# Stick-breaking attention on one core: the scan reads its own score tile, the constant's bank goes to the projections

## Chip, cores, metric

The kernel runs on 1 core of one Trainium2 chip. The metric is the device time of one execution in microseconds (us). PE is TensorE, DVE is VectorE, ACT is ScalarE, POOL is GpSimd, SP is SyncE.

## What is computed

One decoder layer: a modulated RMSNorm, one input projection, an RWKV-7 group and a stick-breaking attention group of 8 heads x 64, an output projection, a final RMSNorm. Sequence 2048, width 1024. The change lies in the attention:

```python
z = jnp.einsum('bhqd,bhkd->bhqk', q_blk, k).astype(jnp.float32) * scale
mask = k_pos[None, :] < q_pos[:, None]
log_1m = jnp.where(mask, jax.nn.log_sigmoid(-z), 0.0)
after = lax.cumsum(log_1m, axis=3, reverse=True) - log_1m
attn = jnp.where(mask, jnp.exp(jax.nn.log_sigmoid(z) + after), 0.0)
return jnp.einsum('bhqk,bhkd->bhqd', attn.astype(v.dtype), v)
```

With u = sigmoid(-z) and s = sigmoid(z) the weight of a key is s times the product of u over the later allowed keys.

## The kernel before

The program has three stretches: a start (modulation, the normed input h in two float16 parts, the first projections), the attention, and the RWKV group with the output projection. The attention and the RWKV stretch are separate scheduling contexts. In the first, a list scheduler sets the order on every engine from its own estimate of durations; each engine then executes its list strictly in order.

The attention has 16 steps n = 4j + b: j is a pair of heads, b a block of 512 queries. Step n has 8(b + 1) *score tiles* of 128 queries x up to 512 keys, and as many *turns*; 320 of each in all. For a score tile (`scores`): two matmuls write z into one of three PSUM banks (lines 492, 493); ACT makes u and s from z (496, 497); DVE scans u from the last key to the first (505, 508), a running product whose start is in the extra column `u[:, nk]`; POOL multiplies s by the shifted result (509). In a diagonal tile the last 128 keys are masked: POOL zeroes s above the diagonal (502), and the scan takes the maximum with a constant, 1 where the key is not allowed. For a turn (`turn`, `weigh`): PE transposes up to four 128 x 128 pieces into one of two `tr` banks (521), ACT and DVE split them in a high and a low part (525, 526), and two matmuls add both, weighted with v, to the `av` bank (539, 540). Score tiles run 5 ahead of turns, and `weigh` 3 behind them.

The scan has a second operand, `data1`: the constant `dmask`, which stands in a PSUM bank of its own for the whole attention. With `op1=ALU.bypass` its values are ignored.

Beside the attention, `fill` computes the projections that later steps need: k, q and the gates (24 matmuls with 512 columns each, lines 356 to 358, tiles psk, psq, psg, pss), v (96 matmuls with 128 columns, lines 368 to 370, psv). `_merge` interleaves the two jobs by estimated durations; the scheduler then moves instructions further. All projections of the attention write into the one `mm` bank. It is free again when ACT and DVE have taken the sum out (lines 419 and 420 for k, 405 and 406 for q, 432 and 433 for v, 441 and 442 for a gate). Ahead of the attention `mm_ps` hands out the three z banks instead.

PSUM has eight banks here: mm 1, z 3, tr 2, av 1, dmask 1.

Of the kernel before, what the change touches and what calls it, by code (L numbers as in the profile page):

```python
# [7 lines left out]
F32 = mybir.dt.float32  # L8
# [4 lines left out]
AF = mybir.ActivationFunctionType  # L13
ALU = mybir.AluOpType
# [4 lines left out]
P = 128  # L19
D = 1024  # L20
KB = D // P
TB = 512
# [32 lines left out]
def _merge(*jobs):  # L55
    _run(_side(*jobs))
# [32 lines left out]
def trunk(nc, a, out):  # L89
# [3 lines left out]
    PE, V, A, G, DMA = nc.tensor, nc.vector, nc.scalar, nc.gpsimd, nc.sync  # L93
# [5 lines left out]
    base = -(-nc.sbuf_base // 32) * 32  # L99
# [5 lines left out]
    def dram(name, shape):  # L105
        return nc.dram_tensor(name, shape, F32, kind="Internal").ap()
# [3 lines left out]
    sm = stage.enter_context(tc.tile_pool(name="small", bufs=2))  # L110
    pp = stage.enter_context(tc.tile_pool(name="ps", bufs=2, space=PSUM))

    NM = [1, 3, 2]
    early = [True]

    def mm_ps(name="mm"):
        if early[0]:
            return z_ps(name)
        return pp.tile([P, TB], F32, tag="mm", bufs=NM[0], name=name)

    def z_ps(name="z"):
        return pp.tile([P, TB], F32, tag="z", bufs=NM[1], name=name)

    def tr_ps(name="tr"):
        return pp.tile([P, TB], F32, tag="tr", bufs=NM[2], name=name)

# [84 lines left out]
    for e in range(2):  # L211
# [4 lines left out]
        for m in range(8):  # L216
# [16 lines left out]
                    op0=ALU.bitwise_and)  # L233
# [117 lines left out]
    def inproj(w, b, name):  # L351
        wh, wl = w[0], w[1]
        ps = mm_ps(name)
        for k in range(KB):
            with tc.issue_after(pace[0]) if pace[0] is not None else nullcontext():
                PE.matmul(ps, wh[:, k], hth[b][:, k], start=k == 0, stop=False)  # L356
            PE.matmul(ps, wh[:, k], htl[b][:, k], start=False, stop=False)  # L357
            PE.matmul(ps, wl[:, k], hth[b][:, k], start=False, stop=k == KB - 1)  # L358
            yield 0.65
        return ps  # L360
# [114 lines left out]
    def step(n):  # L475
        if n not in steps:
            b = n % NB
            steps[n] = ([(h, kb) for h in range(2) for kb in range(b, -1, -1)], {}, {}, {})
        return steps[n]

    def scores(n, i, sb):
        j, b = divmod(n, NB)
        groups, att, carry, _ = step(n)
        qt = qst[n]
        gi, q = divmod(i, 4)
        h, kb = groups[gi]
        kt = kst[NB * j + kb]
        diag = kb == b
        nk = (q + 1) * P if diag else TB
        qs = slice(q * P, (q + 1) * P)  # L490
        z = z_ps()
        PE.matmul(z[:, 0:nk], qt[:, h, 0, qs], kt[:, h, 0:nk], start=True, stop=False)  # L492
        PE.matmul(z[:, 0:nk], qt[:, h, 1, qs], kt[:, h, 0:nk], start=False, stop=True)  # L493
        u = sb.tile([P, TB + 1], F32, tag="u", bufs=NU, name="u")
        s = sb.tile([P, TB], F32, tag="s", bufs=NS, name="s")
        A.activation(out=u[:, 0:nk], in_=z[:, 0:nk], func=AF.Sigmoid, scale=-0.125)  # L496
        A.activation(out=s[:, 0:nk], in_=z[:, 0:nk], func=AF.Sigmoid, scale=0.125)  # L497
        ur = u[:, 0:nk][:, ::-1]
        mr = dmask[:, TB - nk:TB][:, ::-1]
        if diag:  # L500

            G.affine_select(out=s[:, nk - P:nk], in_=s[:, nk - P:nk], pattern=[[-1, P]], compare_op=ALU.is_gt,
                            fill=0.0, base=0, channel_multiplier=1)
            G.memset(u[:, nk:nk + 1], 1.0)
            V.tensor_tensor_scan(out=ur, data0=ur, data1=mr, initial=u[:, nk:nk + 1], op0=ALU.mult, op1=ALU.max)  # L505
        else:
            G.tensor_copy(out=u[:, nk:nk + 1], in_=carry[h, q][:, 0:1])
            V.tensor_tensor_scan(out=ur, data0=ur, data1=mr, initial=u[:, nk:nk + 1], op0=ALU.mult, op1=ALU.bypass)  # L508
        G.tensor_tensor(out=s[:, 0:nk], in0=s[:, 0:nk], in1=u[:, 1:nk + 1], op=ALU.mult)  # L509
        carry[h, q] = u  # L510
        att[gi, q] = s
        return 0.45 * nk / TB
# [60 lines left out]
    def attend(n, sb):  # L573

        p0 = seq.index((n, 0))
        p1 = p0 + 8 * (n % NB + 1)
        ahead = LEAD if n % NB else 0
        if n % NB == 1 or n == 0:
            for p in range(p0, p0 + LEAD):
                yield scores(*seq[p], sb)  # L580
        for p in range(p0, p1):
            if p + LEAD < min(p1 + ahead, len(seq)):
                yield scores(*seq[p + LEAD], sb)
            held.append(turn(*seq[p], sb))
            yield 0.43
            if len(held) > LAG:
                weigh(sb, *held.pop(0))
            yield 0.43
        if n == NST - 1:
            while held:  # L590
                weigh(sb, *held.pop(0))
# [41 lines left out]
    def fill(n, sb):  # L633

        j, b = divmod(n, NB)
        end = j == NB - 1
        if n < 2:
            m = n + 2
        else:
            m = n + 1 if 2 < n < NST - 1 else None  # L640
        new = b == 3 and not end
        if b == 0 and j > 0:
            yield from w_split("g", j)
        if b == 2:
            yield from w_split("r", j)
            w_load("z" if end else "k", 0 if end else j + 1)
        if b == 3:
            yield from w_split("z" if end else "k", 0 if end else j + 1)
            w_load("rk" if end else "q", 0 if end else j + 1)
        gates = [("g", 0)], [("g", 1)], [("g", 2), ("g", 3), ("r", 0)], [("r", 1), ("r", 2), ("r", 3)]  # L650
        gates = [proj_g(kind, j, gb, sb) for kind, gb in gates[b]]
        if m is not None:
            yield from proj_k(m)
            if new:
                yield from gates.pop(0)
                yield from w_split("q", j + 1)
                w_load("v", j + 1)
            yield from proj_q(m)
            if new:
                yield from gates.pop(0)  # L660
                yield from w_split("v", j + 1)
                w_load("g", j + 1)
            yield from proj_v(m)
        if j > 0:
            yield from combine(j - 1, b, sb)
        if n == NST - 1:
            for i in range(4):
                yield from proj_z(i, sb)
                if gates:
                    yield from gates.pop(0)  # L670
                if i < 3:
                    yield from w_split(("rk", "rr", "rv")[i], 0)
                if i < 2:
                    w_load(("rr", "rv")[i], 0)
        for g in gates:
            yield from g
        if b == 1:
            w_load("r", j)

    def fill_work(n):  # L680
        b = n % NB
        if n == NST - 1:
            return 5.2 * 7 + 1.5
        return 5.2 * ((4, 4, 6, 6)[b] - 3 * (n == 2)) + 0.9 * (n > 3) + (0.2, 0, 0.2, 0.6)[b]

    dts = []
    early[0] = False
    with tc.tile_pool(name="sb", bufs=2) as sb:

        dmask = pp.tile([P, TB], F32, tag="dmask", bufs=1, name="dmask")  # L690
        dm = sb.tile([P, TB], F32, tag="ot", bufs=1, name="dm")
        G.memset(dm, 0.0)
        G.affine_select(out=dm[:, TB - P:TB], in_=dm[:, TB - P:TB], pattern=[[-1, P]], compare_op=ALU.is_gt,
                        fill=1.0, base=0, channel_multiplier=1)
        A.activation(out=dmask, in_=dm, func=AF.Copy)
        for n in range(NST):
            b = n % NB
            _merge((attend(n, sb), 8.6 + 10.48 * b), (fill(n, sb), fill_work(n)))
            if n == 1:

                zeros = sb.tile([P, TB], F32, tag="ot", bufs=1, name="zeros")
                G.memset(zeros, 0.0)
                for i in range(2):
                    dts.append(dram(f"dt{i}", [2, 2, 8, 65, 64]))
                    for m in range(2):
                        for h in range(2):
                            DMA.dma_start(out=dts[i][m, h].rearrange("c s t -> s c t")[0:64],
                                          in_=zeros[0:64].rearrange("p (c d) -> p c d", c=8))
# [12 lines left out]
    pp = stage.enter_context(tc.tile_pool(name="ps", bufs=2, space=PSUM))  # L721
    NM[:] = [3, 2, 2]
    rwk = stage.enter_context(ExitStack())
# [598 lines left out]
```

## Time and profile before

| | |
|---|---|
| runs | 1924.12 us median of 3 (1922.18 to 1925.9) |
| the profiled execution | 1919.86 us, span 1918.1 us |
| busy in the span | PE 1699.1 us (89%), DVE 1380.4 (72%), ACT 859.7 (45%), POOL 774.4 (40%) |
| attention (137 to 1043 us) | 906 us: PE busy 837, DVE 676, ACT 535, POOL 470 |
[...]

PE counts as busy while a matmul is in its pipeline, so that neighbours overlap; the cost of a matmul in a dense row is the distance between starts. The waits view gives, for each pair of a waiting instruction and the one that released it, the idle time in all, how often, and the longest.

### The profile page before, as it was taken

The numbers are of one execution on the slowest core, as the hardware profiler recorded it, in microseconds if no ns is written. First come the engines' busy times: TensorE is split into PE (matmuls) and PEld (weight loads), VectorE is DVE, ScalarE is ACT, GpSimd is POOL, SyncE is SP. The second block draws the span as 40 slices with busy tenths as digits, with TensorE's granted clock in tenths as the row PEclk, the third lists the DMA queues.
The fourth block names the chain that finished last, engine by engine and source line by source line (L and its number), as shares of the span: only waits on it lengthen the run. The fifth ranks groups of instructions, "written<-read, shape, count | busy, mean of one in ns | idle before, by whom it ended". The sixth has DMA issues, their size and how long they took to land. (4 is left out here: it accounts for less than half of the span.)

```text
span 1918.1 us, 38809 instructions
## 1 busy us (share of the span) xinstructions
PE 1699.1 (89%) x14816; PEld 1164.2 (61%) x14816; DVE 1380.4 (72%) x2871; ACT 859.7 (45%) x1706; POOL 774.4 (40%) x1114
## 2 busy tenths in 40 slices
PE   1879978999899998999997888898899998989998
PEld 1546655666565665667654455665565655667886
DVE  8967697678785778768766557878777777765543
ACT  0556576456564666546644333333332333422221
POOL 3615465356553556445444123233233322223322
PEclk9989999999999999999989989999999999999999
DMA  8341201222122221132111523322332333335442
GB/s 296 112 144 45 70 25 45 64 75 64 42 56 75 61 67 41 51 79 69 54 45 39 154 49 86 69 62 77 77 80 77 86 78 104 80 92 169 149 138 88
DMA packets 210408, 159.93 MB, mean 83 GB/s; under 512 B 113247, under 2 KB 171820, under 8 KB 210222
## 3 DMA queue, kind: packets, MB, share of 16 engines
q1 hardware_dynamic: 209220, 155.31, 28.8%
q8 instruction: 117, 1.92, 0.4%
q10 hardware_dynamic: 1002, 2.13, 0.4%
q14 instruction: 69, 0.57, 0.1%
HBM read 94.48 MB, written 44.04 MB: 72 GB/s over the span
## 5 line engine op out<-in xcount | busy, mean ns | idle before, releaser
L509 POOL TENSOR_TENSOR s<-s,u 128x512 f32<-128x512 f32 (+2 forms) x320 | 306.0, 964 | 219.6 <-ACT s L497 99.7
L526 DVE TENSOR_TENSOR al<-tr,ah 128x512 fp32r<-128x512 f32 (+1 forms) x320 | 187.3, 598 | 98.0 <-ACT ah L525 97.2
L508 DVE TENSOR_TENSOR_SCAN u<-u,dmask 128x512 f32<-128x512 f32 x192 | 239.8, 1267 | 13.7 <-ACT u L496 12.1
L525 ACT ACTIVATE ah<-tr 128x512 fp32r<-128x512 f32 (+1 forms) x320 | 171.9, 553 | 104.8 <-PE tr L521 101.5
L496 ACT ACTIVATE u<-z 128x512 f32<-128x512 f32 (+2 forms) x320 | 173.4, 556 | 73.4 <-PE z L493 48.1
L521 PE MATMUL tr<-kept_ident,s 128*128 128x128 f32 x1088 | 174.2, 280 | 32.8 <-DVE al L526 26.2
L497 ACT ACTIVATE s<-z 128x512 f32<-128x512 f32 (+2 forms) x320 | 166.2, 549 | 54.6 <-PE tr L521 54.6
L521 PEld LDWEIGHTS tr<-kept_ident,s 128*128 128x128 f32 x1088 | 130.9, 143 | 74.5 <-DVE al L526 37.5
L356 PE MATMUL pss<-kept_hh,kept_wh 128*128 128x512 f16 x416 | 160.4, 386 | 8.8 <-PEq L716 8.8
L357 PE MATMUL pss<-kept_hl,kept_wh 128*128 128x512 f16 x416 | 160.3, 385 | 0.0
L358 PE MATMUL pss<-kept_hh,kept_wl 128*128 128x512 f16 x416 | 160.3, 385 | 0.0
L358 PEld LDWEIGHTS <-kept_wl 128*128 128x128 f16 x928 | 93.3, 101 | 105.1 <-issue 14.2
L356 PEld LDWEIGHTS <-kept_wh 128*128 128x128 f16 x928 | 94.5, 102 | 101.5 <-issue 29.8
L357 PEld LDWEIGHTS <-kept_wh 128*128 128x128 f16 x928 | 93.3, 100 | 92.8 <-issue 23.1
L492 PE MATMUL z<-kt,qt 128*128 128x512 f32 (+2 forms) x320 | 132.2, 418 | 10.4 <-ACT s L497 4.4
L539 PE MATMUL av<-ah,vt 128*128 128x512 f32 (+1 forms) x320 | 136.6, 427 | 4.8 <-DVE o L550 2.3
L540 PE MATMUL av<-al,vt 128*128 128x512 f32 (+1 forms) x320 | 136.3, 427 | 0.2 <-DVE al L526 0.2
L493 PE MATMUL z<-kt,qt 128*128 128x512 f32 (+2 forms) x320 | 117.5, 371 | 0.0
L505 DVE TENSOR_TENSOR_SCAN u<-u,dmask 128x128 f32<-128x128 f32 (+3 forms) x128 | 107.2, 866 | 12.2 <-ACT u L496 6.6
L356 PE MATMUL psg<-kept_hh,kept_wh 128*128 128x512 f16 x256 | 100.4, 392 | 8.2 <-DVE klo L420 3.1
L1260 PE MATMUL po<-kept_woh,kept_yh 128*128 128x512 f32 x256 | 103.3, 404 | 0.0
L1261 PE MATMUL po<-kept_wol,kept_yh 128*128 128x512 f32 x256 | 101.9, 398 | 0.0
(292 smaller groups left out, 4167.0 us busy)
## 6 DMA issues: line engine op xcount, KB each, us to landing
kept_raw<-in_w_in SPq DMA_DIRECT2D x29, 512.0 KB, 3.9
ad<-in_ada_w SPq DMA_DIRECT2D x24, 512.0 KB, 5.4
qt<-qt SPq DMA_DIRECT2D x48, 256.0 KB, 3.4
xt<-in_x SPq DMA_DIRECT2D x16, 512.0 KB, 5.2
y<-sg SPq DMA_DIRECT2D x32, 256.0 KB, 2.0
t<-dt SPq DMA_DIRECT2D x64, 128.0 KB, 3.1
xr<-in_x SPq DMA_DIRECT2D x16, 512.0 KB, 3.6
out<-xr SPq DMA_DIRECT2D x16, 512.0 KB, 2.6
```

Source lines behind the costliest of these rows:

```text
L356: PE.matmul(ps, wh[:, k], hth[b][:, k], start=k == 0, stop=False)
L357: PE.matmul(ps, wh[:, k], htl[b][:, k], start=False, stop=False)
L358: PE.matmul(ps, wl[:, k], hth[b][:, k], start=False, stop=k == KB - 1)
L496: A.activation(out=u[:, 0:nk], in_=z[:, 0:nk], func=AF.Sigmoid, scale=-0.125)
L497: A.activation(out=s[:, 0:nk], in_=z[:, 0:nk], func=AF.Sigmoid, scale=0.125)
L508: V.tensor_tensor_scan(out=ur, data0=ur, data1=mr, initial=u[:, nk:nk + 1], op0=ALU.mult, op1=ALU.bypass)
L509: G.tensor_tensor(out=s[:, 0:nk], in0=s[:, 0:nk], in1=u[:, 1:nk + 1], op=ALU.mult)
L521: PE.transpose(tp[:, q * P:(q + 1) * P], att[gi, q][:, ks * P:(ks + 1) * P], ident)
L525: A.activation(out=ah[:, r], in_=tp[:, r], func=AF.Copy)
L526: V.tensor_tensor(out=al[:, r], in0=tp[:, r], in1=ah[:, r].bitcast(F32), op=ALU.subtract)
L539: PE.matmul(av[:, r], vs, ah[:, r], start=first, stop=False, skip_group_check=True)
L540: ins = PE.matmul(av[:, r], vs, al[:, r], start=False, stop=last, skip_group_check=True)
```

## The change

The scan of every tile now has `data1 = z`, the score tile's own bank, and always `op1=ALU.bypass`; `dmask` is gone. A diagonal tile is masked ahead of the scan: POOL's `affine_select` sets u to 1 and s to 0 above the diagonal. The bank that held `dmask` is a second `mm` bank, and `mm_ps` hands out `mm` banks from the start.

```diff
-    NM = [1, 3, 2]
-    early = [True]
+    NM = [2, 3, 2]
 
     def mm_ps(name="mm"):
-        if early[0]:
-            return z_ps(name)
         return pp.tile([P, TB], F32, tag="mm", bufs=NM[0], name=name)
...
         ur = u[:, 0:nk][:, ::-1]
-        mr = dmask[:, TB - nk:TB][:, ::-1]
         if diag:
 
-            G.affine_select(out=s[:, nk - P:nk], in_=s[:, nk - P:nk], pattern=[[-1, P]], compare_op=ALU.is_gt,
-                            fill=0.0, base=0, channel_multiplier=1)
+            for t, f in ((u, 1.0), (s, 0.0)):
+                G.affine_select(out=t[:, nk - P:nk], in_=t[:, nk - P:nk], pattern=[[-1, P]], compare_op=ALU.is_gt,
+                                fill=f, base=0, channel_multiplier=1)
             G.memset(u[:, nk:nk + 1], 1.0)
-            V.tensor_tensor_scan(out=ur, data0=ur, data1=mr, initial=u[:, nk:nk + 1], op0=ALU.mult, op1=ALU.max)
         else:
             G.tensor_copy(out=u[:, nk:nk + 1], in_=carry[h, q][:, 0:1])
-            V.tensor_tensor_scan(out=ur, data0=ur, data1=mr, initial=u[:, nk:nk + 1], op0=ALU.mult, op1=ALU.bypass)
+
+        V.tensor_tensor_scan(out=ur, data0=ur, data1=z[:, 0:nk][:, ::-1], initial=u[:, nk:nk + 1],
+                             op0=ALU.mult, op1=ALU.bypass)
...
-    early[0] = False
     with tc.tile_pool(name="sb", bufs=2) as sb:
-
-        dmask = pp.tile([P, TB], F32, tag="dmask", bufs=1, name="dmask")
-        dm = sb.tile([P, TB], F32, tag="ot", bufs=1, name="dm")
-        G.memset(dm, 0.0)
-        G.affine_select(out=dm[:, TB - P:TB], in_=dm[:, TB - P:TB], pattern=[[-1, P]], compare_op=ALU.is_gt,
-                        fill=1.0, base=0, channel_multiplier=1)
-        A.activation(out=dmask, in_=dm, func=AF.Copy)
```

Since banks come free at other moments, the scheduler writes another order for the start and the attention on every engine. The instructions are the same but for the scan's operand, 128 selections more on POOL, and the making of `dmask`. The order of the RWKV stretch is unchanged.

PE near the end of step 6 (j = 1, b = 2), around turn 120 of 320. In these rows tr is a turn's transposes, z the scores, av the weighting, psg a gate's projection. Before:

```order
L358 MATMUL psg<-kept_hh_987,kept_wl_799 128x512
L356 LDWEIGHTS kept_wh_798
L356 MATMUL psg<-kept_hh_987,kept_wh_798 128x512
L357 LDWEIGHTS kept_wh_798
L357 MATMUL psg<-kept_hl_988,kept_wh_798 128x512
L521 MATMUL tr<-kept_ident_61,s 128x128 x3
L358 LDWEIGHTS kept_wl_799
L358 MATMUL psg<-kept_hh_987,kept_wl_799 128x512
L492 MATMUL z<-kt,qt 128x128
L539 MATMUL av<-ah,vt 128x512
L540 MATMUL av<-al,vt 128x512
```

And now, at the same turns:

```order
L519 MATMUL tr<-kept_ident_61,s 128x128 x3
L538 MATMUL av<-al,vt 128x512
L489 MATMUL z<-kt,qt 128x512
L490 MATMUL z<-kt,qt 128x512
L489 MATMUL z<-kt,qt 128x512
L490 MATMUL z<-kt,qt 128x512
L519 MATMUL tr<-kept_ident_61,s 128x128 x2
L489 MATMUL z<-kt,qt 128x128
L490 MATMUL z<-kt,qt 128x128
L519 MATMUL tr<-kept_ident_61,s 128x128
L537 MATMUL av<-ah,vt 128x512
```

The gate's matmuls no longer stand here: they stand among the turns before. From turn 112 to 127 there were 72 matmuls of gates and 9 of v, and there are 12 of gates now; from turn 114 to 132 there is none.

ACT in the same step (u and s are the two sigmoids of a score tile, ah the high part of a turn). Before:

```order
L496 ACTIVATE u<-z 128x512 x2
L525 ACTIVATE ah<-tr 128x512
L496 ACTIVATE u<-z 128x512
L525 ACTIVATE ah<-tr 128x512 x2
L497 ACTIVATE s<-z 128x512 x3
L525 ACTIVATE ah<-tr 128x512 x2
```

And now:

```order
L523 ACTIVATE ah<-tr 128x512
L493 ACTIVATE u<-z 128x512 x3
L523 ACTIVATE ah<-tr 128x512 x2
L494 ACTIVATE s<-z 128x512 x3
L523 ACTIVATE ah<-tr 128x512
```

An s that stands behind an ah, and so behind PE's transposes, is found in 132 of the 320 tiles before and in 136 now. What moved is what hangs on it: in the built program the scan now waits for the tile's s, since both read the same bank; before, it waited for u alone.

POOL at the first diagonal tiles of step 3 (j = 0, b = 3). Before:

```order
L504 MEMSET u 128x1
L509 TENSOR_TENSOR s<-s,u 128x512
L504 MEMSET u 128x1 x2
L509 TENSOR_TENSOR s<-s,u 128x512
L504 MEMSET u 128x1
L502 AFFINE_SELECT s<-s 128x128 x2
L509 TENSOR_TENSOR s<-s,u 128x128
```

And now:

```order
L507 TENSOR_TENSOR s<-s,u 128x512
L499 AFFINE_SELECT u<-u 128x128
L501 MEMSET u 128x1 x2
L507 TENSOR_TENSOR s<-s,u 128x512
L499 AFFINE_SELECT u<-u 128x128
L501 MEMSET u 128x1
L499 AFFINE_SELECT u<-u 128x128
L499 AFFINE_SELECT s<-s 128x128 x3
L507 TENSOR_TENSOR s<-s,u 128x128
```

The selections on u stand ahead of the products, one for each diagonal tile; before there was only the one on s.

## Rows read from the trace of the kernel before

**Rows 1.** The page: the span, and each engine's busy time.
```profile
span 1918.1 us, 38809 instructions
PE 1699.1 (89%) x14816; PEld 1164.2 (61%) x14816; DVE 1380.4 (72%) x2871; ACT 859.7 (45%) x1706; POOL 774.4 (40%) x1114
```
**Rows 2.** Busy time by stretch: start, attention, RWKV (stretch, us, engines, clock, DMA).
```profile
52.50:137.30 84.80, 68.42 (x472) 44.15 (x472) 72.54 (x118) 50.17 (x77) 33.72 (x22) 0.94 0.48 145
137.30:1043.00 905.70, 836.67 (x5345) 570.97 (x5344) 676.30 (x1004) 534.81 (x1122) 470.18 (x836) 0.97 0.21 56
1043.00:1918.10 875.10, 785.06 (x8963) 540.78 (x8962) 585.78 (x1653) 272.20 (x502) 250.71 (x229) 0.97 0.35 95
```
**Rows 3.** Waits between 137 and 1043 us: who waits on whom, us, times, longest.
```profile
PEld tr L521 <- DVE al L526: 37.5, 34, 2.5
PE tr L521 <- DVE al L526: 26.2, 26, 2.2
PE psq L356 <- DVE klo L420: 5.2, 3, 1.7
PE psg L356 <- DVE klo L420: 3.1, 2, 1.9
PE psg L356 <- DVE sg L442: 2.9, 1, 2.9
PE psg L356 <- DVE z L389: 2.1, 1, 2.1
PE psv L368 <- DVE qt L406: 2.0, 4, 0.8
```
**Rows 4.** Timeline of PE: spacing of matmuls, and of the last turn.
```profile
354.69 0.48 PE L540 MATMUL av<-al,vt 128*128 128x512 f32 x1
355.01 0.40 PE L492 MATMUL z<-kt,qt 128*128 128x512 f32 x1
355.24 0.40 PE L493 MATMUL z<-kt,qt 128*128 128x512 f32 x1
355.71 0.38 PE L357 MATMUL psk<-kept_hl,kept_wh 128*128 128x512 f16 x1
355.92 0.38 PE L358 MATMUL psk<-kept_hh,kept_wl 128*128 128x512 f16 x1
...
514.08 1.04 PE L521 MATMUL tr<-kept_ident,s 128*128 128x128 f32 x8
...
1041.16 0.66 PE L521 MATMUL tr<-kept_ident,s 128*128 128x128 f32 x4
```
**Rows 5.** Busy time by stretch: turns 96 to 111, 112 to 127, 128 to 151.
```profile
411.50:455.60 44.10, 43.66 (x330) 31.24 (x328) 34.70 (x52) 27.92 (x60) 25.29 (x45) 1.00 0.29 75
455.60:497.10 41.50, 39.63 (x220) 25.79 (x218) 31.90 (x41) 26.57 (x57) 19.48 (x41) 1.00 0.12 40
497.10:560.10 63.00, 55.65 (x278) 36.98 (x277) 52.26 (x80) 39.60 (x81) 36.51 (x56) 0.92 0.18 49
```
**Rows 6.** Timeline of DVE and ACT while PE computes a k and a gate.
```profile
508.54 1.08 ACT L496 ACTIVATE u<-z 128x512 f32<-128x512 f32 x2
510.05 1.26 DVE L508 TENSOR_TENSOR_SCAN u<-u,dmask 128x512 f32<-128x512 f32 x1
512.42 2.44 DVE L508 TENSOR_TENSOR_SCAN u<-u,dmask 128x512 f32<-128x512 f32 x2
515.72 1.28 DVE L526 TENSOR_TENSOR al<-tr,ah 128x512 fp32r<-128x512 f32 x2
520.70 1.09 ACT L497 ACTIVATE s<-z 128x512 f32<-128x512 f32 x2 [4.47 <-PE tr L521]
```
**Rows 7.** Groups by line and shape: busy us, mean ns, idle time before and its releasers.
```profile
L508 DVE TENSOR_TENSOR_SCAN u<-u,dmask 128x512 f32<-128x512 f32 x192 | 239.8, 1267 | 13.7 <-ACT u L496 12.1 <-POOL u L504 0.5
L505 DVE TENSOR_TENSOR_SCAN u<-u,dmask 128x512 f32<-128x512 f32 x32 | 40.6, 1269 | 3.1 <-ACT u L496 2.8
L509 POOL TENSOR_TENSOR s<-s,u 128x512 f32<-128x512 f32 x224 | 245.7, 1103 | 213.2 <-ACT s L497 99.7 <-DVE u L508 51.1 <-ACT u L496 13.1
L502 POOL TENSOR_SCALAR_AFFINE_SELECT s<-s 128x128 f32<-128x128 f32 x128 | 37.9, 301 | 119.9 <-ACT s L497 119.7
```
**Rows 8.** Waits between 137 and 1043 us, of ACT and DVE.
```profile
ACT s L497 <- PE tr L521: 54.6, 35, 6.3
DVE u L505 <- ACT dmask L695: 4.5, 1, 4.5
```

## The prediction
> **What bounds the kernel now.** I read the page first, then the busy times by stretch, then the waits of the attention, then timelines of the few places that the change touches. The page says that PE is busy for 89% of the span and DVE for 72% [rows 1], but that is a mean over stretches with different limits. Cut by stretch [rows 2], the start (84.8 us) is DVE's, with 72.5 us busy against 68.4 for PE; the attention is 905.7 us with PE busy 836.7, DVE 676.3, ACT 534.8 and POOL 470.2; the RWKV stretch, 875.1 us, keeps its order and I carry it over unchanged. [...]
>
> Inside the attention the busy share hides which engine sets the pace, so I price one turn with its score tile. PE: two score matmuls of 0.23 each (start to start: 355.01 to 355.24) [rows 4], four transposes of 0.11 each (eight are through in 1.04, pipeline included), and two weighting matmuls of some 0.24 (taken like the score matmuls, they have the same 512 columns): 2 x 0.23 + 4 x 0.11 + 2 x 0.24 = 1.38 us. DVE: one scan of 1.22 (two in 2.44) and one al of 0.61 to 0.64 (two in 1.28) [rows 6]: 1.83 us. So a turn alone is DVE's, and 0.45 us of other PE work per turn, about two projection matmuls at 0.21 (355.71 to 355.92) [rows 4], make it PE's. The attention is as fast as it is because the projections are spread over the turns. How evenly they are spread is what the scheduler's new order changes.
>
> **Accumulator waits, removed.** With one mm bank PE waits until DVE has taken the sum out. The waits of PE on klo, sg, z and qt are 5.2 + 3.1 + 2.9 + 2.1 + 2.0 = 15.3 us [rows 3]. A second bank can take all of it. **-15.** Its bounds: 0, if PE then waits for tr banks at the same places (the waits for al are the largest there are, 26.2 us on PE and 37.5 on its weight load), and -15.
>
> **Balance, changed.** I cut the built order into 40 pieces of 8 turns, multiply PE's and DVE's instructions in each by the durations above, and take the larger of the two sums as the piece's time. That gives 804 us before and 831 after: **+27**. Pieces of 16 turns give +18, of 4 turns +31; these are the bounds I keep. By pair of heads it is +9, +11, +11 and -5. The tally is 90 us short of the trace (turns run from 145 to 1042 us, 897 us, the last transposes at 1041.16 [rows 4]), since waits and slower clock are not in it; I assume that these stay. One place shows how it comes about. In turns 112 to 127 PE had 72 gate matmuls: 16 turns at 1.38 (22.1) + 72 x 0.216 (15.6) + small ones of v make 38.3 us against 34.1 for DVE, where the trace has 41.5 us with PE busy 39.6 [rows 5]. Now 12 gate matmuls remain, 23.8 us for PE, and DVE with 30.5 decides: 7.8 us less. But the 60 matmuls, 13 us, went into turns 72 to 111, which were already PE's: 114.3 us there become 127.6. Net +5.5 us. Then in turns 128 to 151 two projections stand in a row (some 41 matmuls, 9 us of PE with nothing for DVE to do but their takes) where single chunks of 22 to 24 stood, and in the turns after them DVE needs 18.3 us for what takes PE 12: 51.3 becomes 56.7. In the trace this is the stretch of 63.0 us with PE at 55.7 and the clock at 0.92 [rows 5]; more idle PE can cost more clock here, which is not in the term and is one reason for the upper end.
>
> **The scan's new wait.** Scan and second sigmoid s now read the same bank, and the scan waits for s. Before, DVE ran ahead: the scans at 510.05 and 512.42 were done while the s came at 520.70, after 4.47 us of ACT's waiting for transposes [rows 6]. ACT waits in front of s on PE 35 times, 54.6 us [rows 8], because an ah stands before it. Now what is queued behind the scan on DVE waits too: the al of the next turns, which free tr banks, for which PE waits already [rows 3]. Bounds: 0, if the scans that ran early had slack of as much, and 35 scans of 1.27 [rows 7] that can't be done in those waits, 44 us. Most of that DVE work is found again in PE-bound turns, where DVE has 0.2 to 0.4 us to spare per turn: I take **+8**, nearer the low end because in the stretch as a whole DVE is idle 229 of 905.7 us [rows 2].
>
> [...]
>
> **z held longer, selections on u.** A z bank is now free only after its scan (three banks, some 1.25 us later where u and s used to release it), and 128 more selections of 0.30 stand ahead of the diagonal scans: 37.9 us of POOL's time [rows 7], which takes POOL from 470 to 508 of 906, not to a bound. The scan then waits for POOL where it waited for ACT, and what is queued behind it is al again; 0.3 us in 128 tiles is 38 at most, 0 at least. Score tiles run 5 ahead of turns and POOL is idle nearly half of the stretch: **+3**. The scan itself keeps its price: with max it took 1269 ns, with bypass 1267 [rows 7], and its second operand came from PSUM before too.
>
> **The start.** The wait for dmask goes, 4.5 us of DVE once [rows 8]. Against it k(1) and q(1), 48 matmuls or 10.4 us, moved from the start, where DVE was the bound and PE had room, to a later place, and the start has two accumulators instead of three. These can go either way by 2: **0**.
>
> **Sum.** -15 + 27 + 8 + 3 + 0 = +23 us on the profiled execution of 1919.9, that is 1943; the median of the runs shown is 4.3 us above that execution, so 1947 on the median's footing (1924.1 + 23). From the bounds of balance (+18 to +31), of the wait (0 to about +20 as far as I believe it within this case) and of the selections, the forecast's own range is 1928 to 1964.
>
> **Rivals.** *The accumulator waits decide* and the balance costs nothing: the score tiles' lead of 5 lets PE and DVE drift apart by some 8 us, enough to smooth pieces of 8 turns. The 90 us that the tally lacks speak for it, and so does the last pair, where the tally gains by itself; against it speaks that turns 128 to 151 show idle PE in the trace today [rows 5]. Then -15 remains: 1909, faster. It decides if PE's idle time for al doesn't grow. [...]
>
> *The scans behind s decide*: DVE is the later engine in most of the turns where ACT waits for transposes, so the 44 us are paid in full, beside a lead that is lost: -15 + 27 + 44 + 2 = +58, 1982. For it: al is already what PE waits for most. Against it: DVE's idle share in the attention is 25%.
>
> *It cancels*: the waits saved pay for what the order costs, within 0.2% or 3.8 us, which is also about what a measurement of this kernel can tell from no change. The four terms would have to halve together.
>
> **Chances.** Forecast 0.55, accumulator waits 0.20, cancelling 0.10, scans behind s 0.15. Faster by over 0.2% is 0.20, within it 0.10, slower 0.70. The range goes from 1910, just past the faster case, to 1982, which leaves out about 2 in 10 in all (the lower tail of the first rival and the upper half of the last).
>
> **What would show it.** Right: PE's waits for klo, sg and qt are gone; around turns 113 to 133 PE is idle on al and the sums of 26.2 and 37.5 us grow; DVE's idle time in front of the scan is put down to ACT's s; the attention is some 23 us longer than 905.7 and the last stretch again 875. Wrong: an attention under 900 us with PE's share above 0.92 (the balance was no cost), or PE's waits on al unchanged while scans wait on s (then the lead covers it). If the scan's mean changes from 1.27 us, the second operand has a price that I put at nothing.

## The result and the profile after

The changed kernel takes 1940.53 us in the median (1930.53 to 1941.98, 6 runs), the kernel before 1923.28 (1917.13 to 1925.9, 6 runs). The ratio is 1.0085, 95% interval 1.0065 to 1.0104: it is slower, by some 16 us. The profiled execution has a span of 1938.6 us against 1918.1.

The page of the changed kernel, span and busy times, which answers to [rows 1]:

```profile
span 1938.6 us, 39034 instructions
...
PE 1721.6 (89%) x14816; PEld 1157.2 (60%) x14816; DVE 1381.3 (71%) x2871; ACT 868.5 (45%) x1705; POOL 808.5 (42%) x1240
```

Busy time by stretch of the changed kernel, cut as in [rows 2] (start, attention, RWKV; stretch, us, engines in the order PE, PEld, DVE, ACT, POOL, clock, DMA):

```profile
52.50:137.30 84.80, 66.11 (x454) 43.59 (x453) 69.97 (x119) 50.61 (x82) 35.08 (x33) 0.84 0.50 140
137.30:1062.30 925.00, 861.00 (x5364) 564.42 (x5363) 681.70 (x1000) 543.44 (x1116) 502.82 (x952) 0.98 0.20 55
1062.30:1938.60 876.30, 784.95 (x8961) 540.37 (x8959) 583.40 (x1652) 271.92 (x502) 250.64 (x229) 0.97 0.35 94
```

Nearly all of it lies in the attention: 925.0 us for 905.7 (+19.3), while the last stretch takes 876.3 for 875.1. DVE has the same work (682 us for 676) and POOL 33 us more, where it has the selections on u.

The waits view of the changed kernel between 137 and 1062 us (who waits on whom, us, times, longest), which answers to [rows 3] and [rows 8]:

```profile
PEld z L489 <- DVE u L505: 72.4, 93, 2.6
...
DVE u L505 <- ACT s L494: 42.1, 43, 3.2
PE z L489 <- DVE u L505: 39.9, 70, 2.1
...
PEld tr L519 <- DVE al L524: 20.7, 48, 2.7
...
ACT s L494 <- PE tr L519: 11.0, 16, 2.0
...
PE tr L519 <- DVE al L524: 7.6, 10, 2.3
```

Read the first and third line first, since they are new: PE waits for a *scan* before it can write a score. Where it waited for al (26.2 us, and 37.5 on the weight load), it now waits for a free z bank (39.9 and 72.4). The scan waits for s, 42.1 us in 43 places. PE's waits for klo, sg and qt ahead of psq, psg and psv are gone. So the rows have moved the way that the terms say, but they don't tell what each is worth: whether the scheduler's new order costs time, or the waits, can't be read from one kernel in which both changed. The experiments hold one and change the other.

### The profile page after: what moved, and what is told of

Same layout as the page of the kernel before. It is cut to its first block, busy times and chain, and to the rows that moved or that the text cites. A ratio compares the mean times of both kernels' runs of the same rounds, so it can differ in the third digit from the quotient of the medians.

```text
span 1938.6 us, 39034 instructions
## 1 busy us (share of the span) xinstructions
PE 1721.6 (89%) x14816; PEld 1157.2 (60%) x14816; DVE 1381.3 (71%) x2871; ACT 868.5 (45%) x1705; POOL 808.5 (42%) x1240
## 5 line engine op out<-in xcount | busy, mean ns | idle before, releaser
L505 DVE TENSOR_TENSOR_SCAN u<-u,z 128x512 f32<-128x512 f32 (+2 forms) x320 | 345.4, 1109 | 67.7 <-ACT s L494 42.1
L489 PE MATMUL z<-kt,qt 128*128 128x512 f32 (+2 forms) x320 | 143.1, 449 | 44.8 <-DVE u L505 39.9
L353 PEld LDWEIGHTS <-kept_wh 128*128 128x128 f16 x928 | 94.2, 101 | 98.8 <-issue 26.2
L537 PE MATMUL av<-ah,vt 128*128 128x512 f32 (+1 forms) x320 | 142.9, 446 | 4.3 <-DVE o L548 3.0
L490 PE MATMUL z<-kt,qt 128*128 128x512 f32 (+2 forms) x320 | 118.9, 372 | 0.0
L489 PEld LDWEIGHTS z<-kt,qt 128*128 128x128 f32 x320 | 61.8, 193 | 89.3 <-DVE u L505 72.4
L1252 PE MATMUL po<-kept_woh,kept_yl 128*128 128x512 f32 x256 | 101.6, 397 | 0.0
```

What stands on the lines that cost most here:

```text
L505: V.tensor_tensor_scan(out=ur, data0=ur, data1=z[:, 0:nk][:, ::-1], initial=u[:, nk:nk + 1], op0=ALU.mult, op1=ALU.bypass)
```

## Experiments

**How the order is held.** In most runs the order of the instructions is not left to the scheduler. A table of numbers, taken from another kernel's built program, chains each engine's instructions with edges that set the order and wait for nothing:

```diff
+        ins = [i for i in nc.cur_bb.bb.instructions if i.engine == engine and type(i).__name__ in kinds]
+        for x, y in zip(rows, rows[1:]):
+            tc.add_manual_dep(ins[y], ins[x].name,
+                              mybir.DependencyInfo(mybir.DependencyClass.NoSync, mybir.DependencyReason.DATA),
+                              reason="order")
```

So two kernels can have the same instructions in the same places and differ in one wait or one bank. The traces of z1, p4, p8, p5, p9 and p12 have the same order on every engine, but for the making of the constant and at most ten of PE's 14816 matmuls. All ratios are to the kernel before, run on the same chip; 0.1% is 1.9 us.

### z1: the scan reads z, one accumulator

```diff
-    NM = [2, 3, 2]
+    NM = [1, 3, 2]
```

with `early` and the z banks as accumulators in the start, as before. One bank stays empty.

> The changed kernel with a single accumulator in the attention (one PSUM bank stays empty) and the z banks as accumulators in the start, as before; the scan reads z, and the order is the scheduler's own. The tally of its order (larger of PE and DVE over pieces of 8 turns) is that of the kernel before. By the prediction the balance's cost is gone and no accumulator wait is saved: 0 + 8 + 3, so +5 to +15 us. By the rival (scan's wait and held bank carry the loss, the second bank only helps): +17 + 15, so +25 to +35 us.

1.0115 (1.0087 to 1.0143), +22 us. That lies between the two expectations. z1 is as slow as the changed kernel, although the tally of its order (PE against DVE over 8 turns) is that of the kernel before. What makes it slow, the next group tells.

### p4 and p8: the same order, without the scan's waits, and with one of them

p4 has z1's order on all four engines, and puts a constant in the empty bank:

```diff
+        dmask = pp.tile([P, TB], F32, tag="dmask", bufs=1, name="dmask")
+        V.memset(dmask, 0.0)
...
-        V.tensor_tensor_scan(out=ur, data0=ur, data1=z[:, 0:nk][:, ::-1], initial=u[:, nk:nk + 1],
+        V.tensor_tensor_scan(out=ur, data0=ur, data1=dmask[:, 0:nk][:, ::-1], initial=u[:, nk:nk + 1],
```

> The order of the one-accumulator kernel (z1) on all four engines, but the scan's ignored operand is a constant in the eighth PSUM bank again, so that it waits for u and POOL alone and z is free once u and s are made. The one-accumulator kernel is 22 us slower than the kernel before, with the same tally. If the scan's waits (s, and z held until the scan) make that loss, it goes: within 5 us of the kernel before. If the order that the scheduler writes around those waits makes it, it stays: +15 to +22 us.

p8 is p4 with a dependency of the scan (`sc`) on its tile's s (`sa`):

```diff
+        tc.add_manual_dep(sc.ins, sa.ins.name, mybir.DependencyInfo(mybir.DependencyClass.Sync,
+                                                                    mybir.DependencyReason.DATA), reason="s")
```

> As the kernel with the constant back in the order of z1, but the scan has an added dependency on its tile's s: it waits for s, while z is still free once u and s are made. If the wait for s makes the loss of the one-accumulator kernel, this one is within 5 us of it (+17 to +27 against the kernel before); if the bank held until the scan makes it, this one is within 5 us of the kernel with the constant back.

p4: 1.0003 (0.9988 to 1.0018). p8: 1.0088 (1.0069 to 1.0107). Same instructions, same order: with neither wait the loss is gone, with the wait for s alone +16 us are back. The remaining 5 us up to z1 are what is left for the z bank that is held until the scan; the intervals of p8 and z1 overlap, so this part is not told from nothing. The selections on u stand in p4 too: its order and they cost nothing together, but what either does by itself can't be told from p4.

The waits view in the attention shows where the wait for s goes. p4:

```profile
PE tr L522 <- DVE al L527: 24.0, 32, 1.8
...
DVE u L508 <- POOL u L502: 20.8, 25, 2.9
...
ACT s L497 <- PE tr L522: 15.9, 11, 4.3
...
DVE u L508 <- ACT u L496: 15.2, 11, 2.6
```

p8:

```profile
DVE u L508 <- ACT s L497: 45.9, 48, 4.2
PE tr L524 <- DVE al L529: 36.4, 40, 2.5
...
ACT s L497 <- PE tr L524: 18.8, 16, 4.3
...
DVE u L508 <- POOL u L502: 6.9, 10, 2.3
```

z1, where z is held as well:

```profile
DVE u L508 <- ACT s L497: 47.5, 48, 4.2
PE z L492 <- DVE u L508: 32.4, 57, 2.2
...
ACT s L497 <- PE tr L522: 16.6, 12, 4.3
...
PE tr L522 <- DVE al L527: 7.1, 10, 1.7
```

In p8 the scan's waits on POOL and on u turn into waits on s and grow from 36.0 (20.8 + 15.2) to 52.8 us (45.9 + 6.9); behind the scan stands al, and PE's wait for al grows from 24.0 to 36.4. In z1 the same lateness comes out as PE's wait for a z bank. The engine that the wait names has changed with the bank that is last; the time hardly has (1.0088 in p8, 1.0115 in z1).

### p5: the second bank in an unchanged order

z1's order on all four engines, with two accumulators in the attention:

```diff
+    NM[0] = 2
```

> The order of the one-accumulator kernel (z1) on all four engines, with two accumulators in the attention; the scan reads z. Only the second bank differs from z1. By the prediction's first term 15 us of PE's waits go: +5 to +10 us against the kernel before. If the second bank gives nothing without a new order, it stays at +18 to +24.

1.0017 (1.0004 to 1.0031), against 1.0115 for z1: the bank is worth 19 us, a little more than expected. Busy time in the attention, from the first transpose to the last weighting, of z1 and then of p5:

```profile
143.10:1067.90 924.80, 860.14 (x5337) 569.04 (x5338) 681.76 (x999) 536.25 (x1115) 503.06 (x952) 0.98 0.20 55
```

```profile
140.70:1049.10 908.40, 850.68 (x5337) 563.74 (x5337) 680.94 (x999) 535.75 (x1115) 503.13 (x952) 0.98 0.20 56
```

Of the 16 us between them 7 are idle time of PE and 9 busy time, at the same matmuls. The 7 fit z1's listed waits on accumulators, some 6 us (psg on klo 3.2, psq on klo 1.8, and small ones). The 9 fit the clock: by the clock record of the traces, z1's attention spends 45.9 us at a granted clock of 0.50 and p5's 27.3. What a microsecond there costs, a place of the kernel before shows, where the granted clock is 0.50:

```profile
287.32 0.63 PE L357 MATMUL psg<-kept_hl,kept_wh 128*128 128x512 f16 x1
287.75 0.63 PE L358 MATMUL psg<-kept_hh,kept_wl 128*128 128x512 f16 x1
```

The starts are 0.43 us apart, against 0.21 where it is 1.00 (355.71 to 355.92 in [rows 4]). So half of the 18.6 us, 9 us, is the most that the clock can have cost here. It is not an accident of one execution: the mean granted clock is 0.967 to 0.974 in z1's six runs and 0.973 to 0.980 in p5's twelve. This share belongs to the price of the bank, since only the bank differs, but the waits view does not list it.

p5 is also the changed kernel in another order: same operands, same banks, same selections. The start differs too, since p5 still takes z banks as accumulators there, but the turns begin at 140.7 us in p5 and at 141.0 in the changed kernel. So 1.0017 against 1.0085, 13 us, is the price of the order that the scheduler wrote. Busy time by stretch, of the changed kernel in turns 96 to 111, 112 to 127 and 128 to 151, as in [rows 5]:

```profile
414.00:468.10 54.10, 54.10 (x355) 34.20 (x354) 39.27 (x58) 30.05 (x63) 27.55 (x52) 1.00 0.25 70
468.10:502.80 34.70, 30.15 (x145) 21.44 (x144) 27.30 (x36) 24.83 (x50) 18.77 (x41) 0.90 0.09 31
...
502.80:568.60 65.80, 58.07 (x282) 35.17 (x280) 52.98 (x81) 40.40 (x81) 40.06 (x62) 0.97 0.18 47
```

And of p5 in the same turns:

```profile
409.20:456.70 47.50, 44.63 (x323) 30.75 (x321) 34.64 (x52) 27.31 (x59) 27.45 (x50) 1.00 0.27 71
456.70:499.10 42.40, 39.68 (x204) 24.81 (x205) 30.84 (x41) 26.89 (x54) 19.83 (x44) 1.00 0.11 38
499.10:562.50 63.40, 57.84 (x282) 35.04 (x281) 52.77 (x81) 40.03 (x81) 38.83 (x61) 0.97 0.18 48
```

In the changed kernel the first stretch is all PE (54.1 of 54.1 busy) and the second is neither engine's in full, with PE at 30 of 34.7 and a granted clock of 0.90 in the mean (0.50 for 6.8 us of it and 1.00 for the rest, where before it was 1.00 throughout); p5 has PE busy 44.6 and 39.7 in stretches of 47.5 and 42.4. That is the imbalance of the prediction, at its place. But these 56 turns differ by 1.3 us in all, since the gain of the second stretch nearly pays for the first, and all 320 by 12.9: by pairs of heads, 80 turns each, by 7.8, 4.9, 1.5 and -1.4, where the prediction has +9, +11, +11 and -5. The clock can have at most 5 us of the 12.9 (37.5 us at a granted clock of 0.50 against 27.3). That the order costs 13 us is shown; that the balance of PE and DVE is what costs them is not.

### p1 and p7: the order of the kernel before

p1 is the changed kernel with PE's matmuls, from the first score on, in the order of the kernel before; the other engines are scheduled around it.

> The changed kernel, but PE's matmuls from the first score on stand in the order of the kernel before (the other engines are ordered around it). The scan still waits for s, z is still held until the scan, there are two accumulators. Against the kernel before: if the balance of PE's order costs what the prediction says (+27 of its terms, of which the measured +17 leaves some 20), that is gone here and -15 + 8 + 3 remain: between -10 and +3 us. If instead the scan's wait and the held z bank carry the loss (rival), the order changes little and it stays 10 to 25 us slower.

1.035 (1.0324 to 1.0376), +67 us: neither. In its waits between 137 and 1120 us each of the new ones is longer than in the changed kernel (72.4, 39.9 and 42.1 there):

```profile
PEld z L489 <- DVE u L505: 95.6, 119, 3.1
...
PE z L489 <- DVE u L505: 59.0, 83, 2.9
...
DVE u L505 <- ACT s L494: 54.2, 39, 5.1
```

So an order can't be priced apart from the waits that it was written for, which is what both sides had assumed.

p7 has the order of the kernel before on PE, DVE and ACT, its constant and its single accumulator; only the masking is the new one (`data1=dmask`, selections on u and s).

> The order of the kernel before on PE, DVE and ACT, the constant in PSUM and one accumulator as there, but diagonal tiles masked by POOL's selection on u ahead of a scan that bypasses. So the selections alone are added. By the prediction +3 us (0 to 6). If the selections hold up the scans of the diagonal tiles in full, 128 x 0.3 us: up to +38.

1.0082 (1.0063 to 1.0101), +16 us, where 0 to 6 were expected. POOL's own order is left to the scheduler here. The scan comes so close behind u that a selection between them holds it up, and PE's wait for al rises from 26.2 to 36.8 us:

```profile
DVE u L508 <- POOL u L502: 37.5, 44, 2.8
PE tr L522 <- DVE al L527: 36.8, 30, 3.1
```

In z1's order (p4) the scan waits 20.8 us for the same selections, and the kernel takes the time of the kernel before. It is the same lesson from the other side.

### p2, p3 and p12: an operand in SBUF

These were to take the wait away while keeping two accumulators, by giving the scan an operand that nothing has to wait for. p2 is the order of the changed kernel on four engines, p3 that of the kernel before on PE, DVE and ACT:

```diff
-        V.tensor_tensor_scan(out=ur, data0=ur, data1=z[:, 0:nk][:, ::-1], initial=u[:, nk:nk + 1],
+        V.tensor_tensor_scan(out=ur, data0=ur, data1=ur, initial=u[:, nk:nk + 1],
```

p12 has z1's order, two accumulators, and `data1=_bc(zero1[:, 0:1], [P, nk])`, one column of zeros.

> The changed kernel's order on PE, DVE, ACT and POOL, instruction for instruction, but the scan's ignored operand is u itself in SBUF, so that it doesn't wait for s and z is free once u and s are made. Against the kernel before: by the prediction only the terms +8 and +3 go, and the balance stays: +3 to +10 us, some 10 us better than the changed kernel. By the rival (the scan's wait and the held bank carry the loss) it falls to the kernel before or under it, 0 to -15 us.

> The order of the kernel before on PE, DVE and ACT from the first score tile on, the scan's operand u itself, and two accumulators; POOL has the selections on u. So only the second bank and the selections differ from the kernel before in the attention. By the prediction's first term PE's 15.3 us of waits go, less up to 3 for the selections: -15 to -8 us. By the rival reading that PE then waits for tr banks instead: 0 (within 4).

> The order of z1 on all four engines and two accumulators, but the scan's ignored operand is one column of zeros in SBUF, repeated (step 0). No scan waits for s, z is free once u and s are made. Where the operand was u itself in SBUF, the scan took 1482 ns in place of 1267 and POOL's product 1382 in place of 1103. If what costs there is reading a second SBUF operand at all, this stays: scans near 1500 ns and 40 to 65 us over the kernel before. If it is the amount that is read, one column frees it: scans at 1270 ns and, with the second bank's gain and without the waits, 12 to 20 us under the kernel before.

All three are slow: p2 1.0279 (1.0255 to 1.0302), p3 1.0327 (1.0301 to 1.0354), p12 1.0208 (1.0184 to 1.0232). None of them tells of the waits, since another cost came in with the operand. Groups by line and shape of the changed kernel (busy us, mean ns; idle time before):

```profile
L505 DVE TENSOR_TENSOR_SCAN u<-u,z 128x512 f32<-128x512 f32 x224 | 278.7, 1269 | 47.5 <-ACT s L494 33.5 <-POOL u L503 8.7 <-issue 2.6
L507 POOL TENSOR_TENSOR s<-s,u 128x512 f32<-128x512 f32 x224 | 244.3, 1091 | 238.4 <-DVE u L505 213.6 <-DVE kept_uns L325 4.7 <-DVE rkw L329 3.5
```

Of p3:

```profile
L505 DVE TENSOR_TENSOR_SCAN u<-u 128x512 f32<-128x512 f32 x224 | 327.8, 1482 | 47.4 <-POOL u L499 29.5 <-ACT u L493 9.1 <-POOL u L501 4.0
L507 POOL TENSOR_TENSOR s<-s,u 128x512 f32<-128x512 f32 x224 | 306.8, 1382 | 119.0 <-ACT s L494 60.2 <-DVE u L505 30.9 <-ACT vt L429 10.2
```

Of p12:

```profile
L508 DVE TENSOR_TENSOR_SCAN u<-u,kept_zero 128x512 f32<-128x512 f32 x224 | 332.7, 1507 | 22.4 <-POOL u L502 11.9 <-ACT u L496 7.3 <-POOL u L506 1.9
L510 POOL TENSOR_TENSOR s<-s,u 128x512 f32<-128x512 f32 x224 | 323.5, 1454 | 105.6 <-DVE u L508 65.7 <-ACT ah L526 24.2 <-DVE ssq L566 3.6
```

In the mean scan and POOL's product both grow by some 200 to 360 ns, for 224 tiles of each. In p3 the 24 scans of 512 columns with no POOL instruction beside them take 1275 ns in the mean, the 200 others 1507, up to 2676. In p12 it is 1275 for 22 and 1532 for 202, so that one repeated column costs as much as a whole tile. In the changed kernel 176 scans have POOL beside them and take 1267. One place of p3, DVE and then POOL (start us, us):

```profile
699.53 4.43 DVE L505 TENSOR_TENSOR_SCAN u<-u 128x512 f32<-128x512 f32 x3
```

```profile
699.20 0.29 POOL L499 TENSOR_SCALAR_AFFINE_SELECT u<-u 128x128 f32<-128x128 f32 x1 [0.81 <-ACT u L493]
699.44 0.18 POOL L503 COPY u<-u 128x1 f32<-128x1 f32 x1
699.68 1.22 POOL L499 TENSOR_SCALAR_AFFINE_SELECT s<-s 128x128 f32<-128x128 f32 x1
700.98 1.89 POOL L507 TENSOR_TENSOR s<-s,u 128x512 f32<-128x512 f32 x1
702.82 1.11 POOL L503 COPY u<-u 128x1 f32<-128x1 f32 x1
```

Three scans take 4.43 us in place of 3.8; beside them a selection takes 1.22, where the one that starts ahead of them takes 0.29, and a copy of one column 1.11, where the one that starts ahead of them takes 0.18.

### p9: one more buffer for s

p5 with nine buffers for s (and one for sg).

```diff
-    NS, NU, LEAD, LAG = 8, 5, 5, 3
+    NS, NU, LEAD, LAG = 9, 5, 5, 3
```

> As p5 (order of z1, two accumulators, the scan reads z), with nine buffers for s in place of eight (and one for the gates' sg in place of two, to make room). If the s that the scan waits for is late because its buffer is still read by transposes, the waits of s on PE (15 us there) and of the scan on s (43 us) fall and the time goes 5 to 15 us under p5, that is 2 to 12 us under the kernel before. If s is late because it stands behind other work on ACT, it stays within 3 us of p5.

1.0022 (1.0005 to 1.0039), as p5. The waits of s for its buffer (its releaser is a transpose) fall from 14.8 to 8.2 us, the scan's waits on s only from 42.7 to 40.2. The buffer is not the main thing that makes s late.

### b22 and b12: the bank taken from the scores

The constant stays, and the scan is that of the kernel before. The second accumulator's bank is the third z bank:

```diff
-    NM = [1, 3, 2]
+    NM = [1, 2, 2]
...
     early[0] = False
+    NM[0] = 2
```

> The kernel before with the bank for the second accumulator taken from the scores: two z banks and two accumulators, the constant kept, the scan with max as before; own order. If a second accumulator is worth 19 us wherever it is, and a third z bank little: 5 to 19 us under the kernel before. If three z banks are needed for DVE to run ahead: 10 to 40 us over it.

b12 is the same without the last line: two z banks, one accumulator, one bank empty.

> The kernel before with two z banks in place of three and one bank empty; one accumulator, own order. It tells what of the 40 us that two accumulators with two z banks gained is the accumulator's. If the second accumulator makes them, this one is no faster than the kernel before: 0 to +15 us. If the other order that two z banks bring makes half or more of them, it is 20 us or more under the kernel before.

b22: 1879.72 us, 0.979 (0.977 to 0.981), 40 us under the kernel before, twice what was expected at most, and the fastest version here. b12: 0.9973 (0.9953 to 0.9993). So the third z bank was worth nothing (-5 us without it), and the second accumulator, together with the order that the scheduler writes for it, is worth 35 us where no scan has to wait for s. In b22 and b12 no order is held, so these 35 us are not divided between the bank and its order. Busy time in the attention, from the first transpose to the last weighting, of the kernel before:

```profile
145.30:1043.70 898.40, 831.87 (x5331) 567.45 (x5330) 672.98 (x998) 530.25 (x1109) 466.91 (x823) 0.98 0.21 56
```

and of b22:

```profile
145.90:1003.20 857.30, 814.77 (x5216) 544.61 (x5215) 670.98 (x995) 535.14 (x1111) 468.01 (x816) 1.00 0.22 59
```

The attention is 41 us shorter at the same DVE time, PE idles 42.5 us in place of 66.5, and the clock is at 1.00. The attention spends 6.8 us at a granted clock of 0.50 here, 13.7 in b12 and 42.7 in the kernel before; with half of each difference as the most that the clock can give, it has up to 18 of the 41 us against the kernel before, but only some 3 of the 40 us by which b12's attention (897.1 us) is longer. (Some PE work, 10 us by the matmuls that its order has ahead of the first turn, went into the start.) Its waits between 137 and 1005 us:

```profile
PEld tr L521 <- DVE al L526: 37.9, 42, 2.1
...
PE tr L521 <- DVE al L526: 23.8, 32, 1.6
```

These are the waits for al of the kernel before [rows 3]; the waits for accumulators are gone and no others have come.

## Why the prediction was right, and where it was not

Forecast +23 us (1947), measured +16 (1940.5): right in sign and near in size, but in part by luck, since the errors of its terms cancel. From before to after, through z1's order, the runs give each term; the steps add up to the whole by construction, so this is a division along one path, and p1 and p7 show that another path would divide it differently. By the intervals of the ratios each step is known to some 5 us, those with z1 in them to some 6, the last row to 3.

| step | forecast | measured | from |
|---|---|---|---|
| the second accumulator | -15 (-15 to 0) | -19 | p5 - z1 |
| the scheduler's order (balance) | +27 (+18 to +31) | +13 | after - p5 |
| the scan's wait for s | +8 (0 to +44) | +16 | p8 - p4 |
| z held until the scan | +3 (0 to 38), with the selections on u | +5 | z1 - p8 |
| the start, z1's order and the selections on u, together | 0 for the start | +1 | p4 - before |

- **Balance** is the term that was mis-sized: 13 us for 27, just under its lower bound of 18. The places were right, against p5 as against the kernel before: turns 72 to 111 are longer (135.0 us, p5 126.1, before 123.0), turns 112 to 127 shorter (34.7, p5 42.4, before 41.5), turns 128 to 151 longer (65.8, p5 63.4, before 63.0). Of the net 5.5 us that turns 72 to 127 were to cost, 5.2 are there against the kernel before, where all terms are mixed, but only 1.2 against p5, where the order alone differs. The tally takes the larger of two sums in pieces of 8 turns as if no work could be shifted over a piece's edge; that this is why it is too high is argued, not tested. Nor does it price other orders: it is right for z1's order, whose tally is that of the kernel before (p4 takes the same time), but counted from b22's trace by the same durations it is some 5 us above that of the kernel before, and b22 is 40 us faster.
- **The wait for s** was taken near its low end, because DVE is idle for a quarter of the stretch. In z1's order it measured twice that. DVE's idle time in the mean, 25%, did not help where a scan waited: behind the late scan stands al, and PE waits for al (24.0 us in p4, 36.4 in p8). The reason given for the lateness, that an ah stands ahead of s on ACT, misreads its row: the 54.6 us are waits of s itself for a transpose, its buffer's reader. The ah before the s of 520.70 had ended when ACT began its 4.47 us of waiting:

```profile
515.64 0.59 ACT L525 ACTIVATE ah<-tr 128x512 fp32r<-128x512 f32 x1
```

  The trace of the changed kernel shows what ACT does while scans wait those 42.1 us for s: it works on s for 20.6 us and on u for 11.4, waits in front of a u for scores for 11.0 and in front of s for a transpose for 3.4, and works on ah for 1.6 (instructions overlap a little). So for the most part s is late because ACT makes it behind several u, as in the order shown ahead of the prediction, where three s follow three u; the scan used to start as soon as its u was there. Whether an ah further ahead made the whole row late was not tested.
- **The held z bank** has its rows (39.9 us on PE, 72.4 on the weight load), the largest new waits in the profile, and by z1 - p8 costs some 5 us, not told from nothing. The prediction expected PE's waits for al to grow instead; they fell from 26.2 to 7.6. PE waits for the same late DVE at another bank.
- **Accumulator waits**: the rival that these decide gave 1909. It had the term nearly right and the rest wrong. The second bank gave 19 us in p5 and, as far as the bank and not its order made them, the 35 of b22; what made the change slow is what it paid for the bank.
- **Scans behind s decide** (1982): its mechanism is there, at 16 us for 44 in z1's order. How much of p1's +67 us is this wait was not tested.
- **The clock** stands in no term. The profiled attention spends 42.7 us at a granted clock of 0.50 in the kernel before, 37.5 in the changed one, 33.5 in p4, 47.8 in p8, 45.9 in z1 and 27.3 in p5. So it doesn't make the changed kernel slower than the kernel before, but up to half of each difference, 7 us for the wait for s and 9 for the second bank, is part of what these steps cost or gave.

## What to carry to other kernels

Here a bank that was freed by letting the scan read another bank was paid for with a wait, 16 us in z1's order, and the wait itself was longer in one order than in another (42.1 us in the changed kernel, 54.2 in p1): hold the order fixed and change one wait at a time before you believe any term. Before giving up an operand that costs no wait, look for the bank that costs least to lose: here the third z bank was worth nothing, and the second accumulator with its order 35 us. The sum of engine times in pieces found the places of the imbalance, but not its price (27 us for 13); and a lower granted clock can have been part of a price that no wait lists, up to 9 of the second bank's 19 us.

## What the runs showed of the hardware

With both of the scan's tensor operands in SBUF, scans and POOL's instructions took longer: 1482 ns in p3 and 1507 in p12 for a scan that takes 1269 in the changed kernel, and 1382 and 1454 on POOL for a product that takes 1091 there. The scans with no POOL work beside them took 1275 ns in both, the others 1507 in p3 and 1532 in p12. One repeated column of SBUF did it as well as a whole tile; with the operand in PSUM, the 176 scans of the changed kernel that have POOL beside them took 1267. Beside the scans of p3 even a copy of one column took 1.11 us, where one that started ahead of them took 0.18. What holds the two engines up, no run shows. The constant's PSUM bank kept this from the kernel before, where the scan took 1267 to 1269 ns [rows 7].
